# Gate projections by seven products, fewer plain gate tiles around the attention, and its PSUM tiles as four places of five banks

## The chip, the core and the metric

The kernel runs on one core of one Trainium2 chip. The metric is the device time of one execution in microseconds (us). An engine here is one of TensorE (PE, with its weight loads as PEld), VectorE (DVE), ScalarE (ACT), GpSimd (POOL) and SyncE (SP); SP and POOL only issue transfers in the part of the program that matters here. Every engine works through its own queue in order and waits there for counts (semaphores) that other engines raise.

## The reference

One layer of a streaming encoder is computed for 1024 new frames of a stream (the prompt) and 64 frames of a running stream (the sample), 1088 frames in all. After an RMS norm, one projection gives convolution inputs, queries, keys, values and two sets of gates:

```python
proj = xn @ w_in                      # 1024 -> 3*512 + 3*512 + 2*1024
cb, cc, ch, q, k, v, ga, gb = jnp.split(proj, splits, axis=-1)
cv, conv_state = causal_conv(cc * ch, conv_prefix, w_conv)
ya = (cb * cv) @ w_conv_out
o, new_k, new_v = attn_fn(heads(q), heads(k), heads(v))
yb = o.reshape(B, L, ATT_DIM) @ w_attn_out
merged = jax.nn.sigmoid(ga) * ya + jax.nn.sigmoid(gb) * yb
return merged @ w_out, conv_state, new_k, new_v
```

Each query attends to its own chunk of 64 frames and the eight chunks before it, with a learned bias, in 8 heads of 64. The residual, a SwiGLU feed-forward part with its own norm, and a last norm follow. All arithmetic is to float32 precision.

## The kernel before

Frames lie along the free dimension (four pieces of 272 in two halves of 544), features on the partitions. A float32 product is made of three products of a high and a low part (`split`, L119: ACT copies the high part, DVE subtracts to get the low one).

**Units.** `run` (L218) makes two 128-row tiles of the projection for all frames by seven products of half size for eight (the scheme of Winograd and Strassen); a product is 4 blocks of the inner dimension by 3 part products by 2 pieces, so a unit has 168 matmuls of 272 columns. The list `units` (L479) holds twelve: q, k, cc, ch, cb, and gb for the first four row tiles of the gate b. The results of gb go to memory (`gb_d`) straight from `b_done` (L593), by SP.

**Plain gate tiles.** The rest of the gates, eight row tiles of a and four of b (`GATES`, L305), is made by `gate` (L756) in four pieces of 24 matmuls of 272 columns each (`product`, L294). A piece has a PSUM bank of the pool `pmm` (three banks), ACT copies it out (L764), POOL stores it in `ga_d` or `gb_d`.

**Attention.** For each head h there are nine blocks t: eight of 128 prompt frames, and the sample (t = 8). In the profile `s` is the PSUM tile of the scores, `p` their exponentials in SBUF, `t` the PSUM tile of the turned (transposed) weights, `pt` its split copy (`pts` for the sample), `pv` the values' PSUM tile, `kd`, `qd`, `vd` the head's keys, queries and values. The steps for a block are

- `scores` (L841): PE multiplies queries by up to 640 keys (L856, L857) into a tile of the pool `patt`; `softmax` (L810): DVE adds the bias, negates and finds the row's extreme (L814, with a short read of the accumulator that gives `mx`), ACT takes exponentials (L824);
- `transposed` (L870), two steps later: PE turns the weights in blocks of 128 (L903; L875 and L878 for the sample) into another tile of `patt`; ACT copies (L121) and DVE subtracts (L122) to split them. After the sample's block the sums of the head are turned too (`rt`, L886);
- `values` (L908), three steps later, for two blocks at a time: PE multiplies by the values (L928; L915 for the sample) into `pv` (one bank); `combine` (L826): ACT copies half of it (L830), DVE adds twice (L831, L832), SP stores `o_d`.

`attention` (L934) yields after each of 75 steps. `patt` has two tiles of two banks each (`bufs=2`, [P, 2, 512]); scores and turned weights take them in turn, and scores of over 512 keys are made as two halves in two banks.

**Order of the work.** The code makes the first two pieces of four gate tiles, then the other two pieces of each, then the remaining gate tiles; after each piece from there on `between` (L954) lets attention go on by `PER` = 2.7 steps. Before the last three tiles (`LAST`, L38) attention is run to its end, its pools are closed, and the loads for the next stage are written down: the first gates (`gates_in`), the convolution's result `u` (L990), the attention's result `ob` (L993) and its factors `rc` (L997). ya (from `u`) and yb (from `ob`) follow, row tile by row tile. The order written in the code is not the order on the engines: a scheduler reorders each engine's instructions when the program is built, and moves gate matmuls forward into places where it expects PE to wait. So the program's own order, shown below, is what counts.

Of the kernel before, what the change touches and what calls it, by code (L numbers as in the profile page):

```python
# [8 lines left out]
F32 = mybir.dt.float32  # L9
# [3 lines left out]
PSUM = bass.MemoryType.PSUM  # L13
DRAM = bass.MemoryType.DRAM

P = 128
# [3 lines left out]
TS = 64  # L20
# [12 lines left out]
HT = T // 2  # L33
HN = HT // 2
KB = [2, 3, 3, 3]
C_CB, C_CC, C_CH, C_Q, C_K, C_V, C_GA, C_GB = 0, 512, 1024, 1536, 2048, 2560, 3072, 4096
PER = 2.7
LAST = 3  # L38
# [26 lines left out]
def encoder_kernel(ctx: ExitStack, tc: tile.TileContext, ins, outs):  # L65
    nc = tc.nc
# [52 lines left out]
    def split(hi, lo, src):  # L119

        act.copy(hi, src)  # L121
        vec.tensor_tensor(lo, src, hi.bitcast(F32), op=ALU.subtract)  # L122
# [181 lines left out]
    PIECES = [(j * HN, HN) for j in range(4)]  # L304
    GATES = [("a", m) for m in range(8)] + [("b", m) for m in range(4, 8)]  # L305
    for g, m in GATES:
# [173 lines left out]
    for nm, u in (  # L480
        ("q", 0), ("q", 1), ("k", 0), ("k", 1), ("cc", 0), ("ch", 0), ("gb", 0), ("cb", 0), ("cc", 1), ("ch", 1),
        ("cb", 1), ("gb", 1),
    ):
        base = {"q": C_Q, "k": C_K, "cc": C_CC, "ch": C_CH, "cb": C_CB, "gb": C_GB}[nm]
        units.append((nm, u, w_in[:, base + 2 * u * P : base + 2 * (u + 1) * P]))
# [106 lines left out]

    def b_done(u):  # L593
        def f(r, h, src, snap):
            s = summed(src, snap)
            nc.sync.dma_start(gb_d[(2 * u + r) * P : (2 * u + r + 1) * P, h * HT : (h + 1) * HT], s)

        return f
# [87 lines left out]

    DONE = {"q": q_done, "k": k_done, "cc": cc_done, "ch": ch_done, "cb": cb_done, "gb": b_done}
    x7 = {p: xn.t[gh] for p, gh in PLAIN.items()} | t1
# [121 lines left out]
    def softmax(s, ps, bias, sm, nm):  # L810

        rows = s.shape[0]
        mx = at_pool.tile([P, 1], F32, tag="mx", name=f"mx{nm}", bufs=3)[:rows]
        vec.tensor_tensor_reduce(  # L814
            out=s if len(ps.shape) == 2 else s.rearrange("p (a b) -> p a b", a=2),
            in0=ps,
            in1=bias if len(ps.shape) == 2 else bias.rearrange("p (a b) -> p a b", a=2),
            scale=-1.0,
            scalar=3e38,
            op0=ALU.add,  # L820
            op1=ALU.min,
            accum_out=mx,
        )
        act.activation(s, s, AF.Exp, bias=mx, scale=-1.0, accum_out=sm)  # L824

    def combine(h, pv, n, tok, nm):  # L826
# [9 lines left out]
        else:  # L836
            for e in range(2):
                c = 512 + e * HT
                nc.sync.dma_start(o_d[h * HD : (h + 1) * HD, c : c + 32], o[:, 32 * e : 32 * e + 32])

    def scores(h, t):  # L841
        q, k, ks, v, vs, bias = heads[h]
        ps = patt.tile([P, 2, 512], F32, tag="att", name=f"s{h}_{t}")
        s = at_pool.tile([P, 640], F32, tag="s", name=f"p{h}_{t}", bufs=4)
        if t < 8:
            nb = min(t + 1, 5)
            k0, n, r = (t - nb + 1) * P, nb * P, P
            q0 = t * P if t < 4 else t * P + TS
        else:
            k, k0, n, r = ks, 0, CACHE + TS, TS  # L850
            q0 = 512
        parts = 2 if n > 512 else 1
        w = n // parts
        for i in range(parts):
            ksl = slice(k0 + i * w, k0 + (i + 1) * w)
            mm(ps[:r, i, :w], q[0][:, q0 : q0 + r], k[:, ksl], start=True, stop=False)  # L856
            mm(ps[:r, i, :w], q[1][:, q0 : q0 + r], k[:, ksl], start=False, stop=True)  # L857
# [4 lines left out]
        softmax(  # L862
            s[:r, :n], ps[:r, :, :w] if parts == 2 else ps[:r, 0, :w], bias[:r, b0 : b0 + n], sm[:r, t : t + 1],
            f"{h}_{t}",
        )
        return s
# [3 lines left out]
    def transposed(h, t, s):  # L870
        tp = patt.tile([P, 2, 512], F32, tag="att", name=f"t{h}_{t}").rearrange("p a b -> p (a b)")
        if t == 8:
            pt = at_pool.tile([P, 2, 5, TS], F32R, tag="pts", name=f"pts{h}", bufs=1)
            for i in range(4):
                nc.tensor.transpose(  # L875
                    tp[:, i * TS : (i + 1) * TS], s[:TS, i * P : (i + 1) * P], ident[:TS, :TS]
                )
            nc.tensor.transpose(tp[:TS, 512 : 512 + TS], s[:TS, 512:576], ident[:TS, :TS])  # L878
            split(pt[:, 0, :4, :], pt[:, 1, :4, :], tp[:, : 4 * TS].rearrange("p (b t) -> p b t", t=TS))
            split(pt[:TS, 0, 4, :], pt[:TS, 1, 4, :], tp[:TS, 512 : 512 + TS])  # L880
# [560 lines left out]
    parts = {}  # L1441
# [149 lines left out]
```

## Time and profile before

| what | us |
|---|---|
| three runs: median (lowest, highest) | 1513.29 (1510.24, 1514.9) |
| the profiled execution: its own time | 1515.91 |
| its span, first to last instruction | 1513.8 |
| first unit's matmul of the last unit (gb, second) to the first plain gate matmul | 314.77 to 335.75 |
| plain gates before attention | 335.75 to 362.94 |
| attention, first scores to the last matmul of the values | 362.94 to 558.7 |
| plain gates after attention | 558.7 to 591.85 |
| ya and yb begin | 591.85 and 597.87 |

The profile is one execution. A row of the timeline is: start, time taken, engine, line, operation, what it writes from what it reads, shapes, count, and in brackets the idle time before it and what ended it. A row of a group gives the count, the busy time and the mean of one. A row of the windows gives, for a stretch of time, the busy time of PE, PEld, DVE, ACT and POOL, the clock that TensorE was granted (1.00 is full), and how busy the transfers were. Matmuls overlap each other, so their pace is read from one start to the next, and not from the time that one takes.

### The profile page before, as it was taken

To read this page: it belongs to the slowest core of one execution; us is meant where nothing else is said; L and a number is where in the kernel's file an instruction comes from. 1 tells how busy PE (TensorE), PEld (TensorE's weight loads), DVE (VectorE), ACT (ScalarE), POOL (GpSimd) and SP (SyncE) were. 2 spreads that over 40 slices of the span, in tenths; PEclk is the share of its full clock that TensorE was granted. 3 is DMA by queue.
4 is the path that set the end of the run, shared out by engine and by line. 5 is a ranking of instruction groups with operands and counts; after the bars stand their busy time and mean duration, and the time that the engine had idled before them with its cause. 6 is when DMAs were issued, how large, how long until landed. Compare 5 with 4: busy or idle time off the path is not lost.

```text
span 1513.8 us, 26451 instructions
## 1 busy us (share of the span) xinstructions
PE 1476.9 (98%) x10178; PEld 1381.1 (91%) x10178; DVE 981.2 (65%) x1843; ACT 682.7 (45%) x1397; POOL 128.7 (9%) x236
## 2 busy tenths in 40 slices
PE   7999999999999999999999999999999999999997
PEld 5799999999999999998889999999999998788886
DVE  6886465642776752763489667666666668857576
ACT  6654433333776752542256444444444445402123
POOL 1210010001111121000100011100001011000000
PEclk9999999999999999999999999999999999999999
DMA  7597524168676529554432434443334449667675
GB/s 233 181 305 245 184 78 135 57 187 234 181 186 176 151 82 293 164 167 145 140 126 77 143 134 152 144 148 120 117 142 157 143 177 317 234 221 235 222 259 202
DMA packets 167518, 264.73 MB, mean 175 GB/s; under 512 B 19008, under 2 KB 103168, under 8 KB 167264
## 3 DMA queue, kind: packets, MB, share of 16 engines
q1 hardware_dynamic: 146736, 198.23, 42.2%
q0 software_dynamic: 19504, 62.71, 11.4%
q10 hardware_dynamic: 1152, 2.10, 0.4%
q8 instruction: 80, 1.31, 0.4%
q14 instruction: 46, 0.38, 0.1%
HBM read 171.06 MB, written 91.92 MB: 174 GB/s over the span
## 4 chain that ended last, share of the span: by engine, by line
PE 79%; DMA 8%; DVE 6%; ACT 3%; issue 3%; SPq 1%; POOL 0%; ACTq 0%; POOLq 0%; DVEq 0%
PE Aa L238 9%; PE Ab L238 9%; PE A L1508 7%; PE Da L238 4%; PE Db L238 4%; PE D L1508 3%; PE Bb L238 2%; PE Ba L238 2%; PE B L1508 2%; PE wo L1066 2%; PE wo L1068 2%; PE wo L1067 2%; PE t L903 2%; PE Ak L238 2%; PE g L300 2%
## 5 line engine op out<-in xcount | busy, mean ns | idle before, releaser
L1508 PE MATMUL A<-ring,ht 128*128 128x512 f32 x528 | 126.6, 393 | 3.6 <-ACT acc L1518 1.9
L1508 PEld LDWEIGHTS A<-ring,ht 128*128 128x128 f32 x528 | 98.8, 188 | 27.2 <-ACT acc L1518 3.2
L300 PE MATMUL g<-xn,whp 128*128 128x272 f32 x384 | 113.2, 295 | 0.0
L301 PE MATMUL g<-xn,whp 128*128 128x272 f32 x384 | 112.0, 292 | 0.0
L302 PE MATMUL g<-xn,wlp 128*128 128x272 f32 x384 | 111.6, 291 | 0.0
L121 ACT CAST ring<-w2r 128x512 fp32r<-128x512 f32 (+1 forms) x78 | 43.4, 587 | 105.7 <-PE A L1508 52.6
L121 ACT CAST hq<-sa 128x512 fp32r<-128x512 f32 x77 | 47.7, 619 | 86.4 <-DVE sa L1239 56.6
L814 DVE CUSTOM_DVE_ANT_0 p<-s,bb 128x640 f32<-128x640 f32 (+5 forms) x72 | 47.5, 661 | 45.5 <-DMA bb<-bias_d 28.6
L1227 POOL DMA_DIRECT2D h_d<-hq x77 | 40.9, 532 | 416.5 <-DVE hq L122 242.1
L122 DVE TENSOR_TENSOR hq<-sa,hq 128x512 fp32r<-128x512 f32 x77 | 53.1, 690 | 33.4 <-ACT hq L121 33.3
L300 PEld LDWEIGHTS g<-xn,whp 128*128 128x128 f32 x384 | 72.6, 189 | 1.0
L302 PEld LDWEIGHTS g<-xn,wlp 128*128 128x128 f32 x384 | 72.6, 189 | 0.5
L301 PEld LDWEIGHTS g<-xn,whp 128*128 128x128 f32 x384 | 72.7, 189 | 0.3
L1508 PE MATMUL D<-ring,ht 128*128 128x512 f32 x264 | 63.9, 393 | 1.3 <-ACT acc L1518 1.3
L122 DVE TENSOR_TENSOR wla<-rawa,wha 128x512 fp32r<-128x512 f32 x56 | 38.5, 687 | 40.5 <-ACT wha L121 40.5
L238 PE MATMUL Aa<-tt,wha 128*128 128x272 f32 x352 | 59.1, 289 | 2.5 <-ACT tt L121 2.5
L1508 PEld LDWEIGHTS D<-ring,ht 128*128 128x128 f32 x264 | 49.5, 188 | 13.1 <-ACT acc L1518 1.8
L122 DVE TENSOR_TENSOR ring<-w2r,ring 128x512 fp32r<-128x512 f32 (+1 forms) x78 | 49.0, 647 | 14.4 <-ACT ring L121 14.2
L238 PE MATMUL Ab<-mg,whb 128*128 128x272 f32 x352 | 58.4, 288 | 0.0
L238 PE MATMUL Aa<-mg,wha 128*128 128x272 f32 x352 | 58.3, 288 | 0.0
L238 PE MATMUL Ab<-tt,whb 128*128 128x272 f32 x352 | 58.2, 287 | 0.0
L121 ACT CAST wha<-rawa 128x512 fp32r<-128x512 f32 x56 | 34.8, 621 | 51.3 <-PE Ab L238 35.3
(519 smaller groups left out, 4368.2 us busy)
## 6 DMA issues: line engine op xcount, KB each, us to landing
h_d<-hq POOLq DMA_DIRECT2D x77, 512.0 KB, 3.5
ht<-h_d SPq DMA_DIRECT2D x154, 256.0 KB, 3.7
rawa<-in_w_ff SPq DMA_DIRECT2D x11, 1024.0 KB, 5.9
rawb<-in_w_ff SPq DMA_DIRECT2D x11, 1024.0 KB, 5.4
w2r<-in_w_ff SPq DMA_DIRECT2D x11, 1024.0 KB, 5.8
qd<-q_d SPq DMA_DIRECT2D x32, 272.0 KB, 4.7
rawp<-in_w_in SPq DMA_DIRECT2D x6, 1024.0 KB, 5.9
u_d<-scr SPq DMA_DIRECT2D x8, 544.0 KB, 4.6
```

The costliest lines, as they stand in the source:

```text
L121: act.copy(hi, src)
L122: vec.tensor_tensor(lo, src, hi.bitcast(F32), op=ALU.subtract)
L238: mm(t[:, j, :HN], w[:, k, :], x[p][:, l, k, j * HN : (j + 1) * HN], start=p in (1, 2, 7) and k == 0 and n == 0, stop=k == 3 and n == 2, s ...
L300: mm(out, a, p, start=k == 0, stop=False)
L301: mm(out, a, q, start=False, stop=False)
L302: mm(out, b, p, start=False, stop=k == kt - 1)
L814: vec.tensor_tensor_reduce(out=s if len(ps.shape) == 2 else s.rearrange("p (a b) -> p a b", a=2), in0=ps, in1=bias if len(ps.shape) == 2 e ...
L903: nc.tensor.transpose(tp[:, i * P : (i + 1) * P], s[:, i * P : (i + 1) * P], ident)
L1066: mm(ps, x(k, 0), wh, start=f, stop=False)
L1067: mm(ps, x(k, 0), wl, start=False, stop=False)
L1227: nc.gpsimd.dma_start(h_d[p, c - 1], hq.rearrange("p i l t -> p (i l t)").bitcast(F32))
L1508: mm(t, ht[k][:, j, x], w[:, l], start=p in (1, 2, 7) and k == 0 and n == 0, stop=k == len(ks) - 1 and n == 2, skip_group_check=p in (6, 5 ...
```

## The change

Three things are changed together.

1. Two more units, `ga` 0 and 1, for the first four row tiles of the gate a; `GATES` keeps rows 4 to 7 of a and b, eight tiles. There are 14 units now, ga after cb in each half of the list, and gb 1 before cb 1.
2. `PER` goes from 2.7 to 6.25 steps for a piece, since only twelve pieces lie between the start of attention and `LAST` in the code (28 before).
3. PSUM: `pmm` has two banks for three. `patt` is one tile `five` of 2560 floats, five banks of 512, and `place` hands out four places of 640 floats in turn, for scores and turned weights; scores are cut where a bank ends. The sums' turn takes the rest of the sample's place. The eighth bank stays with `pv`.

```diff
-PER = 2.7
+PER = 6.25
...
-    GATES = [("a", m) for m in range(8)] + [("b", m) for m in range(4, 8)]
+    GATES = [(g, m) for g in "ab" for m in range(4, 8)]
...
-        ("q", 0), ("q", 1), ("k", 0), ("k", 1), ("cc", 0), ("ch", 0), ("gb", 0), ("cb", 0), ("cc", 1), ("ch", 1),
-        ("cb", 1), ("gb", 1),
+        ("q", 0), ("q", 1), ("k", 0), ("k", 1), ("cc", 0), ("ch", 0), ("gb", 0), ("cb", 0), ("ga", 0), ("cc", 1),
+        ("ch", 1), ("gb", 1), ("cb", 1), ("ga", 1),
...
-    def b_done(u):
+    def gate_rows(dst, u):
         def f(r, h, src, snap):
             s = summed(src, snap)
-            nc.sync.dma_start(gb_d[(2 * u + r) * P : (2 * u + r + 1) * P, h * HT : (h + 1) * HT], s)
+            nc.sync.dma_start(dst[(2 * u + r) * P : (2 * u + r + 1) * P, h * HT : (h + 1) * HT], s)
...
-    pmm = pg_stack.enter_context(tc.tile_pool(name="pmm", bufs=3, space=PSUM, reuse_waits="tile"))
+    pmm = pg_stack.enter_context(tc.tile_pool(name="pmm", bufs=2, space=PSUM, reuse_waits="tile"))
...
-    patt = att_stack.enter_context(tc.tile_pool(name="patt", bufs=2, space=PSUM, reuse_waits="tile"))
+    patt = att_stack.enter_context(tc.tile_pool(name="patt", bufs=1, space=PSUM, reuse_waits="tile"))
...
+    five = patt.tile([P, 2560], F32, name="five")
+    places = [0]
+
+    def place():
+
+        a = places[0] % 4 * 640
+        places[0] += 1
+        return five[:, a : a + 640], [512 - a % 512 + 512 * i for i in range(2)]
+
     def scores(h, t):
         q, k, ks, v, vs, bias = heads[h]
-        ps = patt.tile([P, 2, 512], F32, tag="att", name=f"s{h}_{t}")
+        ps, ends = place()
...
-        parts = 2 if n > 512 else 1
-        w = n // parts
-        for i in range(parts):
-            ksl = slice(k0 + i * w, k0 + (i + 1) * w)
-            mm(ps[:r, i, :w], q[0][:, q0 : q0 + r], k[:, ksl], start=True, stop=False)
-            mm(ps[:r, i, :w], q[1][:, q0 : q0 + r], k[:, ksl], start=False, stop=True)
+        at = 0
+        for end in ends:
+            end = min(end, n)
+            if at < end:
+                mm(ps[:r, at:end], q[0][:, q0 : q0 + r], k[:, k0 + at : k0 + end], start=True, stop=False)
+                mm(ps[:r, at:end], q[1][:, q0 : q0 + r], k[:, k0 + at : k0 + end], start=False, stop=True)
+            at = max(at, end)
...
     def transposed(h, t, s):
-        tp = patt.tile([P, 2, 512], F32, tag="att", name=f"t{h}_{t}").rearrange("p a b -> p (a b)")
+        tp = place()[0]
...
-            tr = patt.tile([P, 2, 512], F32, tag="att", name=f"rt{h}")[:9, 0, :P]
+            tr = tp[:9, 512:640]
```

**How the order on the engines moves.** First PE, in the middle of attention. Before, these are the rows from block 6 of the sixth head to the start of its block 7: scores, turned weights of block 4, values of blocks 2 and 3, then matmuls of a gate tile (`g`).

```order
L856 MATMUL s_6_5699<-kd_5244,qd_0_5238 128x320 [waits DVE_49]
L857 MATMUL s_6_5699<-kd_5244,qd_1_5241 128x320
...
L903 MATMUL t_4_5708<-ident,p_4_5631 128x128 [waits DVE_49]
L903 MATMUL t_4_5708<-ident,p_4_5631 128x128 x4
L928 MATMUL pv_3_5717<-pt_1_5640,vd_5254 128x512 [waits Activation_49]
...
L300 MATMUL g_0_5786<-xn_93,whp_0_5373 128x272
L301 MATMUL g_0_5786<-xn_93,whp_0_5373 128x272
L856 MATMUL s_7_5728<-kd_5244,qd_0_5238 128x320 [waits DVE_49]
```

Now the rows of the fifth head (keys `kd_5089`) from block 7 on, with the sample's scores (`ksd`) at their end. Scores and turned weights all go to the one tile `five`.

```order
L867 MATMUL five<-kd_5089,qd_0_5083 128x512 [waits DVE_49]
L868 MATMUL five<-kd_5089,qd_1_5086 128x512
L867 MATMUL five<-kd_5089,qd_0_5083 128x128
L868 MATMUL five<-kd_5089,qd_1_5086 128x128
L912 MATMUL five<-ident,p_5_5417 128x128 [waits DVE_49]
L912 MATMUL five<-ident,p_5_5417 128x128 x4
L867 MATMUL five<-ksd_5090,qd_0_5083 64x256 [waits DMAHW5_49,DMAHW3_49,DVE_49]
```

No gate matmul stands between them any more. Of the 1152 plain gate matmuls of before, PE's rows have 216 ahead of the first scores, 673 amid attention and 263 behind it; of the 768 of now, 216, 552 and none. The 552 all stand in the first 33 of the 75 steps (to block 5 of the fourth head), in two runs for each step, of some 8 between a block's scores and the turned weights and of some 14 behind these; the other 42 steps have none. What the waits for DVE mean differs too. In the program of before, the turned weights of block 4 wait for the subtraction of the turned weights of block 3, which lay in the same tile of `patt` one step earlier, and the scores of block 7 for the extreme of block 6, whose scores lay in theirs. In the program of now the count that the turned weights of block t - 2 wait for is the one that DVE raises with the extreme of block t, the scores directly ahead of them; and the count that the scores of block t + 1 wait for is the one of the last subtraction of block t - 2, the turned weights directly ahead of them. This holds from the first head's third block to the end, but for the scores behind the turned sums of a head, which wait for ACT's copy of these. The places are 640 floats and the banks 512, so each place shares a bank with the ones on both sides, and scores and turned weights stand in alternate places; the waits are kept by bank.

Next PE at the end of attention: the last values (`pv_8`, the sample of the last head) and what follows. Before:

```order
L915 MATMUL pv_8_6504<-pts_6472,vsd_5940 128x2x64 [waits DMAHW2_49,DVE_49]
L915 MATMUL pv_8_6504<-pts_6472,vsd_5940 128x2x64 x3
L915 MATMUL pv_8_6504<-pts_6472,vsd_5940 128x2x64 [waits DMAHW3_49]
L301 MATMUL g_1_6615<-xn_93,whp_0_6148 128x272
L302 MATMUL g_1_6615<-xn_93,wlp_0_6149 128x272
```

Now:

```order
L924 MATMUL pv_8_6317<-pts_6286,vsd_5905 128x2x64 [waits DMAHW6_49,DVE_49]
L924 MATMUL pv_8_6317<-pts_6286,vsd_5905 128x2x64 x3
L924 MATMUL pv_8_6317<-pts_6286,vsd_5905 128x2x64 [waits DMAHW7_49]
L300 MATMUL ya_0_6770<-u,whp_0_6634 128x272 [waits DMAHW0_49,Activation_49]
L301 MATMUL ya_0_6770<-u,whp_0_6634 128x272
```

Before, 263 gate matmuls stand between attention and ya; now ya comes next, and it reads `u`, whose load stands in SP's queue behind the last stores of attention's result as before.

Last ACT in attention, the exponentials of block 6 (`p_6`) and what is around them. Before:

```order
L121 CAST pt_2_5709<-t_4_5708 128x5x128 [waits PE_49,Activation_49]
L830 COPY ca_1_5722<-pv_3_5717 64x512 [waits DVE_49,PE_49]
L824 ACTIVATE p_6_5700,sm_3564<-p_6_5700,mx_6_5705 128x640 [waits DVE_49]
L121 CAST pt_2_5709<-t_5_5737 128x5x128 [waits PE_49]
L824 ACTIVATE p_7_5729,sm_3564<-p_7_5729,mx_7_5734 128x640 [waits DVE_49,Activation_49]
```

Now:

```order
L831 COPY ca_1_5980<-pv_3_5975 64x512 [waits PE_49]
L825 ACTIVATE p_6_5959,sm_3996<-p_6_5959,mx_6_5964 128x640 [waits DVE_49,Activation_49]
L121 CAST pt_2_5967<-five 128x5x128 [waits PE_49,Activation_49]
L825 ACTIVATE p_7_5986,sm_3996<-p_7_5986,mx_7_5991 128x640 [waits DVE_49]
L121 CAST pt_2_5967<-five 128x5x128 [waits PE_49]
```

The copy of the values' half (`ca`) stands ahead of the block's exponentials, and these ahead of the copy of the turned weights, in both; before, the copy that follows the exponentials of block 6 was of the turned weights of block 5, and now it is of block 4.

More of the change, by code (lines that the diff above doesn't have):

```diff
@@ L480, in encoder_kernel @@
     for nm, u in (
-        ("q", 0), ("q", 1), ("k", 0), ("k", 1), ("cc", 0), ("ch", 0), ("gb", 0), ("cb", 0), ("cc", 1), ("ch", 1),
-        ("cb", 1), ("gb", 1),
+        ("q", 0), ("q", 1), ("k", 0), ("k", 1), ("cc", 0), ("ch", 0), ("gb", 0), ("cb", 0), ("ga", 0), ("cc", 1),
+        ("ch", 1), ("gb", 1), ("cb", 1), ("ga", 1),
     ):
-        base = {"q": C_Q, "k": C_K, "cc": C_CC, "ch": C_CH, "cb": C_CB, "gb": C_GB}[nm]
+        base = {"q": C_Q, "k": C_K, "cc": C_CC, "ch": C_CH, "cb": C_CB, "ga": C_GA, "gb": C_GB}[nm]
         units.append((nm, u, w_in[:, base + 2 * u * P : base + 2 * (u + 1) * P]))
@@ L685, in cache_tile @@
             nc.sync.dma_start(dst[:, l], st[:, l].bitcast(F32))
-    DONE = {"q": q_done, "k": k_done, "cc": cc_done, "ch": ch_done, "cb": cb_done, "gb": b_done}
+    DONE = {"q": q_done, "k": k_done, "cc": cc_done, "ch": ch_done, "cb": cb_done}
+    DONE |= {"ga": lambda u: gate_rows(ga_d, u), "gb": lambda u: gate_rows(gb_d, u)}
     x7 = {p: xn.t[gh] for p, gh in PLAIN.items()} | t1
@@ L814, in softmax @@
         vec.tensor_tensor_reduce(
-            out=s if len(ps.shape) == 2 else s.rearrange("p (a b) -> p a b", a=2),
+            out=s,
             in0=ps,
-            in1=bias if len(ps.shape) == 2 else bias.rearrange("p (a b) -> p a b", a=2),
+            in1=bias,
             scale=-1.0,
@@ L861, in scores @@
         sm = sums[h]
[L862 to L865, printed above, removed]
+        softmax(s[:r, :n], ps[:r, :n], bias[:r, b0 : b0 + n], sm[:r, t : t + 1], f"{h}_{t}")
         return s
@@ L877, in transposed @@
                 )
-            nc.tensor.transpose(tp[:TS, 512 : 512 + TS], s[:TS, 512:576], ident[:TS, :TS])
+            nc.tensor.transpose(tp[:TS, 4 * TS : 5 * TS], s[:TS, 512:576], ident[:TS, :TS])
             split(pt[:, 0, :4, :], pt[:, 1, :4, :], tp[:, : 4 * TS].rearrange("p (b t) -> p b t", t=TS))
-            split(pt[:TS, 0, 4, :], pt[:TS, 1, 4, :], tp[:TS, 512 : 512 + TS])
+            split(pt[:TS, 0, 4, :], pt[:TS, 1, 4, :], tp[:TS, 4 * TS : 5 * TS])
             pts[h, 4] = pt
```

## The prediction

> **What bounds the kernel now.** I read the page first, then windows by stage, then the timeline of one attention step. The page's parts 1 and 5:
>
> ```profile
> span 1513.8 us, 26451 instructions
> PE 1476.9 (98%) x10178; PEld 1381.1 (91%) x10178; DVE 981.2 (65%) x1843; ACT 682.7 (45%) x1397; POOL 128.7 (9%) x236
> ...
> L300 PE MATMUL g<-xn,whp 128*128 128x272 f32 x384 | 113.2, 295 | 0.0
> ```
>
> PE is busy for 98% of the span, and the gate matmuls have no idle time ahead of them. So fewer matmuls are worth their full time, as long as PE stays busy. The windows by stage (units; attention; gates behind attention; the columns are in the front part):
>
> ```profile
> 80.00:324.00 244.00, 242.28 (x1938) 241.12 (x1937) 152.31 (x245) 102.94 (x187) 11.63 (x19) 1.00 0.53 167
> 363.00:558.70 195.70, 192.85 (x1371) 177.67 (x1369) 138.07 (x328) 136.25 (x320) 32.28 (x62) 0.99 0.59 157
> 559.40:591.90 32.50, 32.50 (x261) 32.50 (x260) 2.87 (x4) 8.55 (x21) 4.33 (x8) 1.00 0.91 291
> ```
>
> PE is full in all three. In attention DVE and ACT have 138 and 136 us of work beside PE's 193. What keeps PE full there are the 673 gate matmuls that stand amid attention in PE's order. Their pace comes from the starts of stages on PE:
>
> ```profile
> 314.77 0.66 PE L238 MATMUL Agb<-xn,whgb 128*128 128x272 f32 x4
> ...
> 335.75 0.29 PE L300 MATMUL g<-xn,whp 128*128 128x272 f32 x1
> ...
> 362.94 0.22 PE L856 MATMUL s<-kd,qd 128*128 128x128 f32 x1
> ...
> 557.81 0.92 PE L915 MATMUL pv<-pts,vsd 128*128 128x128 f32 x5
> ...
> 591.85 0.29 PE L300 MATMUL ya<-u,whp 128*128 128x272 f32 x1
> ```
>
> A unit of 168 matmuls takes 335.75 - 314.77 = 20.98 us. The 216 gate matmuls before attention take 362.94 - 335.75 = 27.19 us, .1259 us each. So 673 × .1259 = 84.7 us of attention's 195.7 are gates, and without them PE has (195.7 - 84.7) / 8 = 13.9 us of work for a head.
>
> **The change, part by part.**
>
> *Units for plain tiles.* 384 plain matmuls go (48.3 us), two units come: 2 × 20.98 = +42.0 us ahead of the gates. As work that is -6.4 us. The units' additions and splits on DVE and ACT, eight more stores by SP and two more unit loads lie beside PE in the stage of the first window, where DVE is idle for 92 us and the transfers for nearly half; I take them at nothing, and if that cover were gone they could cost what PE waits there now, 244.00 - 242.28 = 1.7 us. POOL has 16 stores fewer.
>
> *Two banks for three in `pmm`.* A piece is 24 × .126 = 3.0 us, and its copy takes .39:
>
> ```profile
> 350.68 0.39 ACT L764 COPY gst<-g 128x272 f32<-128x272 f32 x1 [4.84 <-DMA ga_d<-gst]
> ```
>
> Two pieces later is early enough; this copy waited for its staging tile, not for its bank. Between nothing and .5 us; I take nothing.
>
> *Which gates still stand in attention.* The order has 216 ahead of attention, as before, 552 in its first 33 steps, and none in the last 42 or behind it. So two covers go: the gates in the second half of attention, and the 263 behind it (33 us).
>
> *The five banks.* By the order's waits, the scores of block t + 1 wait for the last subtraction of the turned weights of t - 2, and these for the extreme of block t. So a step is a closed ring: scores, extreme, turned weights, copy, subtraction, scores. Before, the two chains ran beside each other. The rows of one full step, put together from the timeline (the last two rows are the next hand-over of that kind):
>
> ```profile
> 446.49 0.31 PE L856 MATMUL s<-kd,qd 128*128 128x320 f32 x1
> ...
> 446.94 0.31 PE L857 MATMUL s<-kd,qd 128*128 128x320 f32 x1
> ...
> 447.29 0.82 DVE L814 CUSTOM_DVE_ANT_0 p<-s,bb 128x640 f32<-128x640 f32 x1 [0.90 <-PE s L857]
> ...
> 448.04 0.08 DVE L814 DVE_READ_ACCUMULATOR2_ANT mx<- 128x1 f32 x1
> ...
> 448.21 0.83 ACT L824 ACTIVATE p<-p,mx 128x640 f32<-128x640 f32 x1
> ...
> 448.95 0.19 ACT L824 ACTIVATION_READ_ACCUMULATOR p<-p,mx 128x1 f32 x1
> ...
> 449.11 0.75 PE L903 MATMUL t<-ident,p 128*128 128x128 f32 x5
> ...
> 449.95 0.69 ACT L121 CAST pt<-t 128x640 fp32r<-128x640 f32 x1 [0.81 <-PE t L903]
> ...
> 450.68 0.82 DVE L122 TENSOR_TENSOR pt<-t,pt 128x640 fp32r<-128x640 f32 x1 [0.78 <-ACT pt L121]
> ...
> 455.97 0.82 DVE L122 TENSOR_TENSOR pt<-t,pt 128x640 fp32r<-128x640 f32 x1 [0.57 <-ACT pt L121]
> ...
> 456.85 0.33 PE L903 MATMUL t<-ident,p 128*128 128x128 f32 x1 [0.17 <-DVE pt L122]
> ```
>
> Scores .76 (446.49 to 447.25), hand-over .04, extreme .83 (447.29 to 448.12), hand-over .09, exponentials .93 (448.21 to 449.14), copy .69, hand-over .04, subtraction .82, back to PE .06 (456.79 to 456.85): 4.26 us. The turned weights' .75 lie beside the exponentials, which stand ahead of the copy in ACT's queue, as the order's rows of ACT show. Smaller blocks cost less; the groups over all heads:
>
> ```profile
> L814 DVE CUSTOM_DVE_ANT_0 p<-s,bb 128x640 f32<-128x640 f32 (+5 forms) x72 | 47.5, 661 | 45.5 <-DMA bb<-bias_d 28.6 <-PE s L857 16.1
> ...
> L122 DVE TENSOR_TENSOR pt<-t,pt 128x640 fp32r<-128x640 f32 (+2 forms) x64 | 41.7, 652 | 13.3 <-ACT pt L121 12.4
> ...
> L824 ACT ACTIVATE p<-p,mx 128x640 f32<-128x640 f32 (+5 forms) x72 | 50.9, 706 | 9.3 <-DVE mx L814 8.0
> L824 ACT ACTIVATION_READ_ACCUMULATOR p<-p,mx 128x1 f32 (+1 forms) x72 | 13.6, 188 | 0.0
> ...
> L121 ACT CAST pt<-t 128x640 fp32r<-128x640 f32 (+2 forms) x64 | 35.7, 559 | 19.5 <-PE t L903 18.7
> ```
>
> For a head (an eighth): extremes 47.5 / 8 = 6.0 (the short reads of the accumulator mostly overlap), exponentials (50.9 + 13.6) / 8 less .09 of overlap in each of nine 7.3, copies 35.7 / 8 and some .5 for the sample, which is not in the group, 5.0, subtractions likewise 41.7 / 8 + .6 = 5.8, scores 5.6 (by columns, from .76 for 640), hand-overs 9 × .23 = 2.1. That makes 31.8. Copies of the values (`ca`) ahead of the exponentials in three steps and the turned sums I put at a further 3: 35 us a head, where PE has 13.9 us to do, so it is busy for 40%. What the clock does then, before shows at three places:
>
> ```profile
> 366.40:369.80 3.40, 1.70 (x11) 1.17 (x10) 1.45 (x4) 3.39 (x10) 0.00 (x0) 1.00 1.01 295
> 369.80:373.20 3.40, 3.40 (x14) 3.20 (x14) 1.64 (x5) 1.66 (x5) 0.54 (x1) 0.50 1.12 248
> 598.50:601.90 3.40, 1.30 (x9) 1.05 (x8) 2.56 (x5) 0.69 (x1) 0.00 (x0) 1.00 0.96 328
> 601.90:605.30 3.40, 2.94 (x13) 2.94 (x14) 2.59 (x2) 0.41 (x1) 0.00 (x0) 0.50 0.92 253
> 31.90:35.30 3.40, 2.34 (x18) 2.09 (x19) 3.17 (x5) 0.97 (x3) 0.49 (x1) 1.00 0.16 19
> 35.30:38.70 3.40, 3.40 (x17) 2.73 (x16) 2.60 (x6) 2.82 (x6) 1.28 (x2) 1.00 0.78 272
> ```
>
> A stretch of 3.4 us with PE busy for half of it or less (1.70, 1.30) was followed by one at half the clock; a stretch with 2.34 was not. The half clock makes PE busy again, and the next stretch is full. At half the clock, scores (+.76) and turned weights (+.6 beyond the exponentials) add some 7.5 us to a head: 42.5. Taking turns, a head takes between 35 and 42.5; I take 38 (34 to 43).
>
> The Trainium skill ("TensorE: Matmul & The Clock Gate", Part 1: The HAM clock gate) has the clock halved only after a whole idle window of about 3.4 us; by it every head stays at 35, which is the second rival. The rows above speak against it: PE was idle for 1.70 and 2.10 us in them.
>
> *The sum from the first plain gate to ya.* Before: 591.85 - 335.75 = 256.1 us, and behind ya's start yb waits 3.40 - 1.30 = 2.1 us and runs at half the clock for 2.94 (1.5 lost): 259.7. Now:
>
> - 216 gates: 27.2.
> - 33 steps with gates (3.67 heads): PE has 3.67 × 13.9 + 552 × .1259 = 120.5 us, the ring 3.67 × 35 = 128. The 8 matmuls (1.0 us) in front of the turned weights about cover the extreme (.04 + .83 + .09), the 14 (1.8) behind them about what the copy and the subtraction leave. 128 (121 to 138).
> - 39 steps without gates (4.33 heads) × 38 = 165, and three steps for the last turned weights and values, 7: 172 (153 to 194, from heads of 34 and 43).
> - The end. The 263 matmuls covered the loads of `u`, `ob` and `rc` and the work on them; the rows:
>
> ```profile
> 589.89 1.29 DVE L1000 TENSOR_TENSOR rc<-ob,rc 128x1088 f32<-128x1088 f32 x1 [18.73 <-DMA rc<-rc_d]
> ...
> 605.31 1.10 ACT L121 CAST ob<-rc 128x1088 fp32r<-128x1088 f32 x1 [3.00 <-DVE rc L1000]
> ```
>
> The fourth `ob` is ready at 606.4, 47.7 us behind attention's last matmul (557.81 + .92 = 558.73). ya has 96 matmuls (12.1 us) that can go ahead of it, so up to 35.6 us stay open; the transfers of this stretch share the rings with fewer gate stores, so I take 32 (24 to 36).
>
> Sum 27.2 + 128 + 172 + 32 = 359.2. Difference: 42.0 + 359.2 - 259.7 = +141.5 us, so 1657.4 beside the profiled execution's 1515.9. That stands 2.6 us above the median of the three runs: 1654.8, said as **1655 us**. The low ends together (27.2 + 121 + 153 + 24 = 325.2) give +107.5, 1620.8; the high ends (395.2) +177.5, 1690.8.
>
> **The rivals.**
>
> - *The clock stays full.* Idle pieces of 1 to 2 us between matmuls are then not enough to halve it. Heads 35, gates' steps 124: 27.2 + 124 + (4.33 × 35 + 7 = 158.6) + 32 = 341.8, +124.1: 1637. The stretch at 31.90 speaks for it, the other two against it.
> - *Half the clock throughout.* PE at half speed is busy for 27.8 of 42.5 us, 65%, about as much as in the stretch at 31.90, behind which the clock was full; so it should rise again. Heads 42.5, gates' steps 135, end 35: 27.2 + 135 + 192 + 35 = 389.2, +171.5: 1685.
> - *The waits go by place, not by bank.* Then four places decouple the chains, and a head without gates goes at DVE's pace, 138.07 / 8 = 17.3 us: 27.2 + 121 + (4.33 × 17.3 + 5 = 80) + 32 = 260.2, +42.5: 1555. The order's counts speak against it. On this the Trainium skill ("PSUM — Partial Sum Buffer", PSUM bank collisions raise a hardware error) asks for guards by bank and not by address; no run here shows a collision.
> - *Faster, because only the work counts.* 48 products fewer: -6.4, 1507. It needs gates' steps at 120.5 and, for no change, no more than 259.7 - 42.0 - 27.2 - 120.5 = 70 us for the 39 steps and the end together: heads at PE's own 13.9 (60 us) and an end of 10. Those heads would be below DVE's own 17.3, so I give it next to nothing.
>
> **How the numbers follow.** Alternating clock (the forecast) .45; full clock .25; half clock .18; waits by place .07; only the work counts .02; above 1692 .03, for heads with waits for loads that no row shows. The range from 1618 to 1692 takes in the first three with their bounds and leaves out the rest. About 0.3% (4.5 us) is what a measurement of this kernel tells from no change: faster .02, same .01, slower .97.
>
> **What would show it.** In the profile after: scores that begin right behind the subtraction of the turned weights two blocks back; turned weights that begin behind an extreme; steps of 4.3 to 5.6 us in the last heads with PE busy for under two thirds; stretches at .50 of the clock; attention from first scores to last values near 300 us for 196; ya's first matmul held by the load of `u`, yb by `ob`. It is wrong if the last heads take under 25 us, if PE is full in them, or if the units take more than 21 us each.

## The result, and the profile after

The changed kernel takes 1681.01 us (median of six runs, 1679.02 to 1684.13) beside 1512.97 us for the kernel before on the same chip (six runs, 1510.24 to 1515.84). The ratio is 1.1115 (95% interval 1.1096 to 1.1134): 168 us slower. The profiled execution took 1680.85 us; its page begins with

```profile
span 1679.1 us, 26386 instructions
PE 1544.1 (92%) x10146; PEld 1414.4 (84%) x10146; DVE 1002.0 (60%) x1863; ACT 687.5 (41%) x1395; POOL 120.0 (7%) x220
...
PEclk9999999999998555569999999999999999999999
```

PE has 32 matmuls fewer and yet is busy for 67 us more; the page's row of clock slices shows why: for an eighth of the span TensorE is granted half its clock, and a matmul then counts as busy for up to twice as long (the first matmul of ya below takes .56 us, where the same one took .29 before). The starts of the stages on PE, from the timeline:

```profile
377.93 0.29 PE L300 MATMUL g<-xn,whp 128*128 128x272 f32 x1
...
405.18 0.22 PE L867 MATMUL five<-kd,qd 128*128 128x128 f32 x1
...
524.99 0.29 PE L302 MATMUL g<-xn,wlp 128*128 128x272 f32 x1
...
727.16 1.52 PE L924 MATMUL pv<-pts,vsd 128*128 128x128 f32 x5 [1.18 <-DVE ca L832]
...
741.84 0.56 PE L300 MATMUL ya<-u,whp 128*128 128x272 f32 x1 [13.16 <-DMA u<-u_d]
...
757.90 1.27 PE L300 MATMUL yb<-ob,whp 128*128 128x272 f32 x4 [5.49 <-ACT ob L121]
```

The first plain gate matmul comes 377.93 - 335.75 = 42.2 us later (the two units), and attention takes 323.5 us (405.18 to 728.68) for 195.8. Each of the two new units takes 20.98 us on PE, as one did before; the other .2 us lie ahead of them. Now ya waits 13.2 us for the load of `u` and yb 5.5 us for `ob`; before, ya didn't wait and yb waited some 2.6 us. The windows by stage: steps with gates, steps without, the wait for `u`, and ya and yb up to the start of the next product (`wo`):

```profile
405.18:525.11 119.93, 118.95 (x847) 108.29 (x845) 64.97 (x148) 65.68 (x155) 18.71 (x35) 1.00 0.51 146
525.11:728.68 203.57, 126.38 (x421) 90.56 (x419) 78.44 (x179) 68.76 (x157) 10.25 (x21) 0.56 0.23 60
728.68:741.84 13.16, 0.00 (x0) 0.03 (x1) 0.50 (x2) 4.43 (x10) 0.27 (x1) 0.50 0.73 239
741.84:855.99 114.15, 102.49 (x768) 100.81 (x769) 67.14 (x155) 46.24 (x118) 0.00 (x0) 0.95 0.55 167
```

Here lies most of the loss. In the first 33 steps PE is full at the full clock, at 3.63 us a step. In the other 42 steps, 4.85 us each, no engine is busy even for two thirds of the time, at .56 of the clock. The waits of PE in that second stretch (us in total, times, longest):

```profile
PE five L867 <- DVE pt L122: 52.2, 35, 2.4
PE five L912 <- DVE mx L815: 14.8, 24, 0.9
```

These are the two hand-overs of the ring: scores behind the subtraction, turned weights behind the extreme. Of 203.57 - 126.38 = 77.2 us in which PE stands still, they are 67.0. One step from the timeline:

```profile
611.04 0.58 PE L867 MATMUL five<-kd,qd 128*128 128x256 f32 x1 [1.51 <-DVE pt L122]
...
611.96 0.52 PE L868 MATMUL five<-kd,qd 128*128 128x384 f32 x1
612.52 0.82 DVE L815 CUSTOM_DVE_ANT_0 p<-five,bb 128x640 f32<-128x640 f32 x1 [1.53 <-PE five L868]
...
613.40 1.11 PE L912 MATMUL five<-ident,p 128*128 128x128 f32 x4 [0.93 <-DVE mx L815]
...
614.55 0.59 ACT L121 CAST pt<-five 128x512 fp32r<-128x512 f32 x1 [0.19 <-PE five L912]
615.17 0.69 DVE L122 TENSOR_TENSOR pt<-five,pt 128x512 fp32r<-128x512 f32 x1 [1.82 <-ACT pt L121]
...
615.92 0.79 PE L867 MATMUL five<-kd,qd 128*128 128x512 f32 x1 [1.40 <-DVE pt L122]
```

Read it as a relay: each step begins within .1 us of the end of the one above it, and the last is the first one's successor, 4.88 us later. The scores take 1.44 us (611.04 to 612.48), where they took .76 at the full clock.

The account against before, from the first unit's delay to the start of `wo` (692.60 before, 855.99 now): units +42.2, gates ahead of attention +.1, attention +127.7, the stretch from the last values to ya 13.2 for 33.1 (-20.0), ya to `wo` 114.15 for 100.75 (+13.4): 163.4 of the 165.3 by which the span grew.

### The profile page after: what moved, and what is told of

It is laid out like the page before. It is cut to its first block, busy times and chain, and to the rows that moved or that the text cites. A ratio compares the mean times of both kernels' runs of the same rounds, so it can differ in the third digit from the quotient of the medians.

```text
span 1679.1 us, 26386 instructions
## 1 busy us (share of the span) xinstructions
PE 1544.1 (92%) x10146; PEld 1414.4 (84%) x10146; DVE 1002.0 (60%) x1863; ACT 687.5 (41%) x1395; POOL 120.0 (7%) x220
## 3 DMA queue, kind: packets, MB, share of 16 engines
q1 hardware_dynamic: 147888, 200.46, 37.3%
q10 hardware_dynamic: 1152, 2.10, 0.3%
## 4 chain that ended last, share of the span: by engine, by line
PE 62%; issue 22%; DVE 5%; DMA 4%; ACT 4%; POOL 1%; SPq 1%; POOLq 0%; ACTq 0%; DVEq 0%
PE A L1517 6%; PE Ab L238 6%; PE Aa L238 5%; PE D L1517 3%; PE Db L238 3%; PE Da L238 3%; PE pv L937 2%; PE five L867 2%; PE five L912 2%; PE B L1517 2%; PE five L868 1%; DVE pt L122 1%; PE Ak L238 1%; PE Bb L238 1%; PE Acc L238 1%
## 5 line engine op out<-in xcount | busy, mean ns | idle before, releaser
L815 DVE CUSTOM_DVE_ANT_0 p<-five,bb 128x640 f32<-128x640 f32 (+5 forms) x72 | 48.1, 667 | 95.1 <-PE five L868 58.4
L867 PE MATMUL five<-kd,qd 128*128 128x256 f32 (+3 forms) x104 | 45.6, 444 | 45.0 <-DVE pt L122 44.0
L825 ACT ACTIVATE p<-p,mx 128x640 f32<-128x640 f32 (+5 forms) x72 | 50.7, 704 | 88.0 <-DVE mx L815 87.6
L122 DVE TENSOR_TENSOR pt<-five,pt 128x640 fp32r<-128x640 f32 (+2 forms) x64 | 42.1, 658 | 65.8 <-ACT pt L121 65.8
L867 PEld LDWEIGHTS five<-kd,qd 128*128 128x128 f32 x104 | 25.1, 241 | 60.9 <-DVE pt L122 56.9
L301 PE MATMUL g<-xn,whp 128*128 128x272 f32 x256 | 75.0, 293 | 0.0
L302 PE MATMUL g<-xn,wlp 128*128 128x272 f32 x256 | 74.7, 292 | 0.0
L300 PE MATMUL g<-xn,whp 128*128 128x272 f32 x256 | 74.6, 291 | 0.0
L912 PE MATMUL five<-ident,p 128*128 128x128 f32 x240 | 52.7, 355 | 16.6 <-DVE mx L815 14.8
L1517 PEld LDWEIGHTS D<-ring,ht 128*128 128x128 f32 x264 | 49.5, 188 | 13.2 <-ACT acc L1527 1.8
L912 PEld LDWEIGHTS five<-ident,p 128*128 128x128 f32 x240 | 35.9, 180 | 28.7 <-DVE mx L815 23.8
```

Source lines behind the costliest of these rows:

```text
L300: mm(out, a, p, start=k == 0, stop=False)
L301: mm(out, a, q, start=False, stop=False)
L302: mm(out, b, p, start=False, stop=k == kt - 1)
L815: vec.tensor_tensor_reduce(out=s, in0=ps, in1=bias, scale=-1.0, scalar=3e38, op0=ALU.add, op1=ALU.min, accum_out=mx,)
L867: mm(ps[:r, at:end], q[0][:, q0 : q0 + r], k[:, k0 + at : k0 + end], start=True, stop=False)
L912: nc.tensor.transpose(tp[:, i * P : (i + 1) * P], s[:, i * P : (i + 1) * P], ident)
```

## The experiments

Theory 1 was the prediction's: the ring is there because the places share banks. Theory 2: it is there because the places are one tile. Theory 3: no ring is needed, the missing gate matmuls alone make attention long. Each run's ratio is to the kernel before, measured again beside it.

**Two places that share no bank.** Edit of the changed kernel:

```diff
-    five = patt.tile([P, 2560], F32, name="five")
+    five = patt.tile([P, 2048], F32, name="five")
...
-        a = places[0] % 4 * 640
+        a = places[0] % 2 * 1024
...
-        return five[:, a : a + 640], [512 - a % 512 + 512 * i for i in range(2)]
+        return five[:, a : a + 640], [512, 1024]
```

> The changed kernel, but the one PSUM tile has four banks and two places of two banks each, so that scores and turned weights share no bank any more; order of the code, units, gates and pmm as in the changed kernel. Theory 1 (the ring of waits comes from shared banks, as the prediction said): the ring opens, the 42 steps without gates go from 4.85 us each to about 2.2 (heads at DVE's 17 to 20 us), attention falls from 323 to about 215 us, the time from 1681 to about 1575. Theory 2 (the waits are kept for the whole tile, because it is one tile): the ring stays, and the time stays within 10 us of 1681. The order's counts of this kernel still show the ring, so I expect theory 2. Theory 3 (only the missing gate matmuls matter, not the waits): also 1681, with no ring in the rows: scores that begin before the subtraction.

Measured: 1684.01 us, ratio 1.1104 (1.1060 to 1.1149), the same as the changed kernel's. Its window of the steps without gates, and its waits there:

```profile
526.36:730.79 204.43, 127.29 (x413) 89.56 (x411) 78.60 (x179) 68.86 (x157) 10.22 (x21) 0.56 0.23 60
```

```profile
PE five L867 <- DVE pt L122: 51.9, 35, 2.2
PE five L912 <- DVE mx L815: 15.3, 26, 0.9
```

The ring stands, though from the third block on scores lie in the tile's first two banks and turned weights in its other two. The turned weights still wait for an extreme that reads other banks. Theory 1 falls.

**The same two places as two tiles.** Edit of that kernel:

```diff
-    five = patt.tile([P, 2048], F32, name="five")
+    five = [patt.tile([P, 1024], F32, name=f"five{i}") for i in range(2)]
...
-        a = places[0] % 2 * 1024
         places[0] += 1
-        return five[:, a : a + 640], [512, 1024]
+        return five[places[0] % 2][:, :640], [512, 1024]
```

> The four-bank kernel of the experiment with two places, but the two places are two tiles of the pool instead of two halves of one tile: same banks, same cuts of the scores, same pmm, units and PER. Whole-tile theory: without the ring 414 gate matmuls stand in all steps of attention and 138 stay behind it; attention takes PE's work, 111 + 414 x .126 = 163 us, and some waits, 166; the end has 17 us of cover and some 14 us of waits left: 42 + 27 + 166 + 17 + 14 - 260 = +6 against before, about 1520. Bank theory: no difference to the two places of one tile, about 1684.

Measured: 1538.03 us, ratio 1.0126 (1.0107 to 1.0146). Attention's window:

```profile
403.47:576.41 172.94, 167.44 (x1113) 145.41 (x1111) 131.51 (x322) 127.25 (x302) 24.84 (x48) 0.99 0.62 161
```

Four banks, the same cuts, the same two banks of `pmm`; only the tile is cut in two, and 146 us are gone. This pair shows theory 2. The size was a miss: some 1520 was expected. Attention took 172.9 us for the 166 expected, and the end cost more too: ya begins 17.4 us behind the last values and takes 116.9 us to `wo`, where before takes 100.75. Where the ring is gone the program's order changes too (gates reach to the end of attention again, 138 behind it), so the 146 us hold both: the waits themselves, and the cover that the order drew forward because of them.

**The units alone** (the kernel before with the two units and the eight plain tiles that they leave, its own PSUM, PER 6.25).

> The kernel before with the two units and PER 6.25, but its own PSUM: three banks in pmm, two tiles in patt. The order has 538 gate matmuls amid attention, in nearly all steps, and 14 behind it. Ring theory (1 or 2): no ring, so PE is nearly full in attention: (111 + 538 x .126 = 68) = 179, with some waits 180 to 190 us, no stretch at half the clock there; but the end is bare as in the changed kernel (30 us from the last values to where before has 37, of which 33 were gates), so 42 + 27 + 185 + 31 - 260 = +25 against before: about 1538. Theory 3 (the cover is what is missing): the gates are the same number amid attention as in the changed kernel, so attention is again near 320 us and the time near 1680. If only the count of products mattered: 1507.

Measured: 1539.04 us, ratio 1.0149 (1.0108 to 1.0189).

```profile
406.67:585.82 179.15, 177.01 (x1250) 161.64 (x1248) 133.60 (x327) 132.54 (x312) 29.49 (x56) 1.00 0.60 162
```

With nearly the number of gate matmuls in attention of the changed kernel (538 for 552), but spread over all steps and with two tiles, PE is full and attention takes 177 us. So it isn't the number of gate matmuls in attention that makes it long. Whether steps without any are long of themselves, a run further below shows. The end has no cover here: ya starts 16.1 us behind the last values, and from there to `wo` it takes 116.9 us for 100.75.

**The five banks alone** (the changed kernel with the twelve units, the twelve plain tiles and PER 2.7 of before).

> The changed kernel without its two units and with PER 2.7: the four places and the two banks of pmm alone. The order has 936 gate matmuls amid attention, all in the first 53 of 75 steps, and none behind. Ring theory: the first 53 steps are full of PE work (53 / 9 x 13.9 + 936 x .126 = 200 us), the last 22 steps cost 4.85 us each as in the changed kernel (107 us), the end costs 30: 27 + 200 + 107 + 30 - 260 = +104 against before, about 1617. If the places cost nothing: 1513.

Measured: 1626.49 us, ratio 1.0729 (1.0692 to 1.0767).

```profile
366.96:569.16 202.20, 200.38 (x1430) 182.80 (x1429) 108.35 (x243) 108.71 (x254) 31.44 (x59) 1.00 0.51 142
569.16:673.99 104.83, 65.34 (x222) 46.84 (x220) 40.25 (x91) 35.88 (x82) 6.26 (x13) 0.56 0.21 53
```

Expected were about 1617; attention took the 307 us that were expected. The same picture with more gates: full steps until they run out, and 104.8 / 22 = 4.77 us for each step after that.

**More work, less time.** In the changed kernel every later piece of a gate tile is multiplied twice, into the same bank:

```diff
-            product(ps[:, :n], gate_w[i], xn, o, n)
+            for _ in range(1 if i < 4 and c < 2 else 2):
+                product(ps[:, :n], gate_w[i], xn, o, n)
```

> The changed kernel, with every piece of a gate tile but the first eight multiplied twice into the same bank (the result is the same): 576 matmuls or 72.5 us of useless PE work, of which the order puts 24 ahead of attention and 552 amid it; gates now reach to the 64th of 75 steps. Ring theory: PE's waits in the steps without gates are filled and the clock there is full, so 64 steps take what PE has to do (64 / 9 x 13.9 + 1104 x .126 = 238 us) and 11 steps 4.85 each (53): attention 291 for 323, time about 1681 - 32 + 3 = 1652, faster with more work. If PE's work is what binds: +72.5, 1753.

Measured: 1654.93 us, ratio to before 1.0915 (1.0873 to 1.0958), 26 us below the changed kernel with 72.5 us more of PE work.

```profile
409.15:652.72 243.57, 241.38 (x1714) 219.29 (x1712) 124.36 (x284) 117.81 (x274) 24.84 (x47) 1.00 0.43 112
652.72:699.98 47.26, 29.07 (x106) 20.49 (x104) 19.16 (x43) 16.57 (x38) 4.27 (x9) 0.61 0.14 38
```

Sixty-four covered steps take 3.81 us each, at the full clock and with PE full. So the ring itself is no longer than that when the clock is full; what the steps without gates take beyond that, 1 us or more each, came with the half clock.

**Steps without gates, but with two tiles.** The kernel of the units alone, where the last three gate tiles take their PSUM from the next stage's pool, which is now opened when attention's is closed:

```diff
             att_stack.close()
+            psum2 = pg_stack.enter_context(tc.tile_pool(name="psum2", bufs=5, space=PSUM, reuse_waits="tile"))
+            pools.append(psum2)
...
-            ps = pmm.tile([P, 512], F32, tag="mm", name=f"g{i}_{c}")
+            ps = pools[-1].tile([P, 512], F32, tag="mm", name=f"g{i}_{c}")
...
-    psum2 = pg_stack.enter_context(tc.tile_pool(name="psum2", bufs=5, space=PSUM, reuse_waits="tile"))
```

> The kernel before with the two units and PER 6.25, and the last three gate tiles take their PSUM from a pool that is opened when attention's is closed, so that their 288 matmuls stay behind attention. Amid attention are 264, all in the first 35 steps; the other 37 have none, as in the changed kernel, but scores and turned weights lie in two tiles. Ring theory: a step without gates costs what DVE has to do and a little, 2.2 us, at the full clock: attention 35 / 9 x 13.9 + 264 x .126 = 87 and 40 x 2.2 = 85, 172 us; the end is covered as before: 42 + 27 + 172 + 36 + 4 - 260 = +21, about 1535. If the missing gates alone made the steps long (no ring needed): 4.85 us each, attention 280, about 1640.

Measured: 1545.72 us, ratio 1.0187 (1.0167 to 1.0207), where about 1535 was expected; attention took 173.4 us for the expected 172. The windows with gates (the last gate matmul in attention starts at 487.77) and without, and the timeline of a step without (L906 turns the weights in this kernel):

```profile
405.60:495.00 89.40, 87.02 (x615) 79.28 (x614) 67.43 (x166) 67.69 (x161) 13.38 (x26) 1.00 0.69 181
495.00:579.00 84.00, 59.72 (x350) 45.04 (x348) 63.13 (x154) 57.37 (x134) 9.37 (x19) 0.98 0.45 118
```

```profile
524.35 0.77 PE L906 MATMUL t<-ident,p 128*128 128x128 f32 x5
...
525.20 0.69 ACT L121 CAST pt<-t 128x640 fp32r<-128x640 f32 x1 [0.83 <-PE t L906]
...
525.93 0.82 DVE L122 TENSOR_TENSOR pt<-t,pt 128x640 fp32r<-128x640 f32 x1 [0.80 <-ACT pt L121]
...
526.81 0.77 PE L906 MATMUL t<-ident,p 128*128 128x128 f32 x5 [0.29 <-DVE pt L122]
```

As in the changed kernel no gate fills these steps, and yet a full step takes 2.46 us (524.35 to 526.81) and a head 20.4 (the sample's scores of two heads start at 527.55 and 547.96), and the clock stays full until 576.2, 2.8 us before the end. Theory 3 falls. In this step a shorter loop binds: turn, copy, subtraction, next turn into the same tile. Over the whole window PE stands still for 24.3 us; this hand-over is the largest of its waits (7.6 us), ahead of that of the scores for the extreme (5.5).

**Can the saved products be had at all?** Four further runs were made for that; each keeps two or three tiles and cover at the end. The first is the two-tile kernel with ten plain tiles, one unit of gate a and PER 3.75.

> One unit of the gate a in place of two plain tiles, two tiles for scores and turned weights, two banks in pmm, PER 3.75. The order has 480 gate matmuls amid attention, in all steps, and 264 behind it, as before has 263. All theories in which only waits were lost expect the saved products to show here: PE's work falls by 192 x .126 - 20.98 = 3.2 us, attention 111 + 480 x .126 = 171.4 and some waits: 1510 to 1513 beside 1513 of before. If less than six gate matmuls a step is too little for the two chains, attention stays near 180 and the time goes to about 1520.

Measured: 1529.04 us, ratio 1.0079 (1.0066 to 1.0092): a miss. Attention takes 179.3 us with 480 gate matmuls. From the first plain gate to the first scores it is 31.5 for 27.2, and from the last values to ya 37.3 for 33.1, with one gate matmul more: there PE waits 2.4 and 3.3 us for the copy of a gate piece out of its bank, for which it doesn't wait in before. This kernel has two banks in `pmm`, and some of these copies waited for the store that frees their staging tile.

The next is the two-tile kernel with the last two gate tiles held (`LAST` = 2) and PER 4.7.

> Both units, two tiles, two banks in pmm, and the last two gate tiles held behind attention (192 matmuls, 24 us), with 360 amid it in nearly all steps. Attention: PE's work is 111 + 45 = 156, DVE's 138; I expect 160. The end has 24 us of cover for 33 and about 11 us of waits: 42 + 27 + 160 + 24 + 11 - 260 = +4, about 1517. If PE stayed full to the end it would be 6.4 below before, 1507.

Measured: 1534.42 us, ratio 1.0114 (1.0099 to 1.0129), a miss too: attention 170.6 us, of which PE is busy for 160.4.

Then three tiles of two banks, one bank in `pmm` during attention, both units and PER 6.25, with the last three gate tiles held.

> Three tiles of two banks for scores and turned weights in turn, one bank in pmm (a pool of three more for the eight pieces ahead of attention, given back before it), both units, the last three gate tiles held behind attention; 275 gate matmuls amid it, 277 behind. The chain from turned weights to turned weights (the turn .78, copy .70, subtraction .84, back .05: 2.4 us a step, 20.5 us a head in the last heads of the hold with two tiles) opens, since a turn finds another tile. If that chain was the floor of 170 us under attention in the runs with two tiles: attention 152 (PE 111 + 275 x .126 = 146, DVE 138), 42 + 27 + 152 + 36 + 4 - 260 = +1, about 1514. If the floor is something else (DVE's and ACT's own queues, the single bank of pmm): attention stays at 170 or above, 1533 or more.

Measured: 1534.55 us, ratio 1.0127 (1.0102 to 1.0153).

```profile
408.43:573.39 164.96, 146.94 (x974) 126.90 (x972) 130.63 (x320) 123.63 (x294) 23.05 (x45) 0.99 0.61 159
```

Attention is 8 us below the 173.4 us of the kernel with two tiles and 264 gates, so that loop may have been part of the floor; but the gates moved too (the last one in attention starts at 572.2, 1.2 us before its end), and the pair doesn't tell one from the other. And attention stops at 165, not at 152, with PE, DVE and ACT each idle for 18 us or more. What binds there was not found: PE's waits are spread over DVE, ACT and PE's own issue, no kind above 3.4 us.

The last is the same with one unit, ten plain tiles and PER 3.75.

> As the run with three tiles and both units, but one unit: 465 gate matmuls amid attention, 279 behind it. PE's work in attention 111 + 465 x .126 = 170; if the floor is gone: 172, 21 + 27 + 172 + 35 + 4 - 260 = -1, about 1512, no difference that shows to before. If the single bank of pmm makes each of 20 pieces wait for its copy (about .5 us): +10, 1522.

Measured: 1528.05 us, ratio 1.0078 (1.0049 to 1.0106): above the dearer of the two cases, 1522. Attention takes 177.7 us.

So in all kernels without the ring attention went no lower than 165 us, whatever number of gates between 264 and 538 stood in it. Before hides 84.7 us of gates there and 33 us of loads behind 263 more. With fewer plain tiles attention no longer shrinks by what leaves it: with both units and three tiles it is 30.8 us shorter, where 398 gate matmuls fewer are 50.1 us of work; with one unit and two tiles 16.5, where 193 fewer are 24.3. That is more than the 6.4 or 3.2 us of products that are saved. Other parts of the 12 to 29 us by which the kernels without the ring ended behind before differ from run to run, and weren't followed up. None of them beat it.

## Why the prediction was right, and which terms were off

The sign, the place and the mechanism in time were right: the ring, the lost covers and the stage that pays. The time (1681) lies near the upper end of the range, 26 us above the forecast of 1655. That the range held it is owed to the rival with half the clock, which it took in; the forecast's own account of the clock, alternating, did not come true. Steps with gates that were 8 us shorter than forecast hid a quarter of that error. (The sum's ends give 1621 and 1691; the range as stated is up to 3 us wider.)

- *Units +42.0:* measured 42.2. *Gates ahead of attention 27.2:* 27.25.
- *Steps with gates, 128:* 119.9. PE was full, and its own work, which the prediction put at 120.5, was the whole time. The estimate counted 3.67 whole heads of 35 us; but the first nine steps, with little to turn yet, took 29.6 us (405.18 to the second head's first scores at 434.82). The two heads behind them took 35.3 and 35.0 us with PE full, so the ring at the full clock is no longer than the 35 us that were estimated.
- *Steps without gates, 172:* 203.6, the term that was mis-sized, by 32 us and beyond its own upper end of 194. The failed step is "The half clock makes PE busy again, and the next stretch is full. [...] Taking turns, a head takes between 35 and 42.5; I take 38". The clock did not take turns; it stood at half in 51 of the 57 stretches of 3.41 us from 527.73 on. Heads took 43.5 us (588.98 to 632.48, the scores of one block in two heads that follow each other). The rival with half the clock throughout gave 1685, the nearest number. What spoke against it, that a stretch with PE busy for 2.34 us out of 3.40 was followed by a full one, was read from one that began at the full clock; it says when the clock stays, not when it comes back.
- *The end, 32:* 13.2 until ya, and 13.4 more between ya and `wo` than before, with the 3.6 us that before itself loses there: 30.2.
- The sum by these: 27.25 + 119.9 + 203.6 + 30.2 = 381.0, and 42.2 + 381.0 - 259.7 = 163.5.
- *"The waits are kept by bank" (the front part), and the rival "by place, not by bank":* the ring was read rightly from the counts, its reason wrongly. They are kept for the tile. So the remedy that the bank reading suggests, places without a common bank, changes nothing, as the first experiment shows. What the rival supposed, that four places leave the chains free, was false too. The section of the Trainium skill's page "PSUM — Partial Sum Buffer" on bank collisions, which asks for guards by bank, neither explains the ring nor speaks against two tiles.
- *"Only the work counts":* it needed heads of 13.9 us; even without the ring, in the two-tile kernel's steps without gates, a head took 20.4.
- *"Two banks for three in `pmm`", taken at nothing:* true of the changed kernel, where the 216 gates ahead of attention took 27.25 us as before. With one unit and two tiles PE waited 5.7 us for the copies; that a third bank would have spared it wasn't tried there.

The 146 us between the two-place and the two-tile kernel are the price of the ring with what it does to the order; the rest of the 168 us is the price of fewer plain tiles: the kernels with both units and two tiles stand 21 (pmm with two banks) and 23 us (with three) above before.

## What to carry to other kernels

Before cutting a buffer into more places, see what the waits are kept by: four places in one tile gave fewer free steps than two tiles, and the waits can be read in the built program before anything runs. Work that looks like mere load on the busiest engine can be cover: count what a saving uncovers at each place where PE would wait, and keep the saving only where another chain isn't within reach of it. And where a chain of short hand-overs leaves TensorE half idle, price it at the half clock too: once a gap has brought that clock, the chain can keep it.

## What the runs showed of the hardware

TensorE's clock goes up at another share of work than it goes down at. Stretches of 3.41 us set on its changes (window rows of the changed kernel; the third number from the end is the clock):

```profile
524.32:527.73 3.41, 1.61 (x11) 1.15 (x10) 2.20 (x5) 2.20 (x5) 0.05 (x1) 1.00 0.49 155
527.73:531.14 3.41, 3.27 (x10) 2.79 (x11) 0.92 (x3) 0.09 (x1) 0.49 (x1) 0.50 0.57 193
531.14:534.56 3.42, 1.01 (x8) 0.78 (x7) 1.93 (x3) 2.01 (x4) 0.00 (x0) 1.00 0.08 19
...
606.24:609.65 3.41, 3.11 (x9) 2.01 (x9) 1.38 (x3) 1.16 (x2) 0.00 (x0) 0.50 0.00 1
609.65:613.06 3.41, 1.44 (x4) 0.93 (x4) 1.66 (x4) 0.72 (x3) 0.00 (x0) 0.50 0.08 19
...
616.48:619.89 3.41, 3.41 (x13) 2.82 (x11) 1.01 (x3) 0.80 (x2) 0.00 (x0) 0.50 0.00 0
619.89:623.30 3.41, 1.02 (x6) 0.53 (x4) 2.03 (x4) 1.30 (x3) 0.00 (x0) 1.00 0.08 19
```

In these steps without gates a stretch at half the clock with PE busy for 3.2 us or more was followed by a full one, and one with 3.14 or less was not; at the full clock 1.61 us or less brought the half. Over the profiles of all twelve kernels, in stretches of the clock's own record, the two edges are less sharp. At half the clock less than 2.86 us was never followed by the full clock and more than 3.28 always; in between 19 stretches were and 15 were not. At the full clock less than 1.53 us was always followed by the half and more than 1.88 never; in between 15 were and 26 were not. In the steps without gates of the kernel with two tiles, PE's stretches held between 2.10 and 3.02 us of work and the clock stayed full, until one with 1.76 brought the half. So with PE busy for 60 to 80% both states last: which one a kernel is in depends on how it came there. In the changed kernel the stretch with 1.61 us (the first row), where the gates run out, brought the half clock; after it the full clock came back for six stretches, one at a time. The Trainium skill ("TensorE: Matmul & The Clock Gate", Part 1: The HAM clock gate) has the half clock come after an idle window and the full one after a busy window of some 3.4 us. The way up agrees with the 2.86 us and more here; for the way down the measurement decides, for PE had been busy for up to 1.88 us of such a window.
